# Attention scores: the second matmul of a chunk contracts only the 64 rows that hold the high part of the queries

## The chip, the cores and the metric

The kernel runs on one core of one Trainium2 chip. The metric is the device time in microseconds of one execution, all transfers included. A core has a tensor engine (PE; its weight loads are listed apart as PEld), a vector engine (DVE), a scalar engine (ACT), GpSimd (POOL) and SyncE (SP), which here issues nearly all DMAs.

## The reference

A trunk of two layers over a sequence of 1024 with a width of 1024, in float32: an RG-LRU block and a SwiGLU feed-forward, then stick-breaking attention with 16 heads of 64 and another feed-forward, each with an RMS norm ahead. The change concerns the scores `z` of the attention:

```python
def stick_breaking_attention(x, w_qkv, w_o):
    qkv = jnp.einsum("bsd,de->bse", x, w_qkv).reshape(bsz, seq, 3, N_HEADS, HEAD_DIM)
    ...
    for blk in range(seq // Q_BLOCK):
        ...
        z = jnp.einsum("bhqd,bhkd->bhqk", qb, kb).astype(jnp.float32) * scale
        ...
        log_fail = jnp.where(strict, jax.nn.log_sigmoid(-z), 0.0)
        suffix = lax.cumsum(log_fail, axis=3, reverse=True) - log_fail
        weights = jnp.where(strict, jnp.exp(jax.nn.log_sigmoid(z) + suffix), 0.0)
        outs.append(jnp.einsum("bhqk,bhkd->bhqd", weights.astype(vb.dtype), vb))
    ...
    return jnp.einsum("bse,ed->bsd", o, w_o)
```

## The kernel before

The kernel multiplies in a reduced float32 format (`F32R`). To keep the precision of float32, an operand is held as a high part, rounded to that format, and a low part, what the rounding left over. A full product of two split operands is three matmuls, high by high, high by low and low by high (`mm3`, lines 140 to 143).

**Scores.** A head has only 64 dimensions, half the 128 rows that PE contracts. The kernel uses the free half for the split. For head `hx` (0 or 1) of head pair `q`, the tile `Q[q][hx]` of 128 by 1024 holds the queries' high part in 64 of its rows and their low part in the other 64. For `hx` 0 the high part lies in rows 0 to 63 (`top`), for `hx` 1 in rows 64 to 127 (`bot`). `KH[q][hx]` holds the high part of the keys twice, in both halves, and `KL[q][hx]` the low part of the keys twice. So one matmul of `Q` by `KH` (line 1388) gives high by high and low by high, and a second of `Q` by `KL` into the same PSUM tile (line 1389) adds high by low and low by low. Both have the same stationary operand, a block of 128 queries; each matmul has its own weight load.

**Chunks.** `z_part` computes the scores of one chunk: 128 queries by up to 512 keys. `chunk_list` makes 12 chunks for a head, 192 in all: 96 have 512 columns, 32 have 384 and 64 have 256. `z_rest` then takes the sigmoids (ACT, lines 1408 and 1409), the running product along the keys (DVE scan, lines 1412 and 1414) and the product that gives the weights (POOL, line 1415).

**Order.** PE, ACT, DVE and POOL run in the order in which the program is written (`manual_schedule`). The loop at lines 1527 to 1540 does for each step `u`: the score pair of chunk `u + 8` (`LEAD` is 8), the transposes of the weights for unit `u + 2` (up to four, line 1426) and their split, the rest of the chunk, two steps of filling work, and the two matmuls of weights by values of unit `u` (lines 1447 and 1448). Filling work is mostly `qkv_steps`, the projections of the next head pair, three matmuls of 512 columns a step (lines 141 to 143). All matmuls other than line 1389's keep 128 rows in before and after. Score tiles come from a PSUM pool of two, so a chunk's first matmul waits until ACT has read the chunk two back.

**Moves.** `qkv_steps` makes the queries, keys and values of a head pair in halves of 512 positions. It splits the product into `th` (high) and `tl` (low), each 128 rows for the two heads, and copies 64-row halves into `Q`, `KH` and `KL` by DMAs from SP's queue (`move`, defined at line 1348; each is 64 by 512 float32, 128 KB). For the keys these are eight moves a half, lines 1354 to 1356. `th` and `tl` have one buffer each, so the next split waits until the moves out of it have landed.

Of the kernel before, what the change touches and what calls it, by code (L numbers as in the profile page):

```python
# [33 lines left out]
def trunk(  # L34
# [22 lines left out]
    nc = tc.nc  # L57
# [53 lines left out]
    def load_raw(src, shape):  # L111
        raw = rp.tile([P, D], F32, tag="raw", name="raw")
        view = raw if len(shape) == 1 else raw.rearrange("p (a b) -> p a b", a=shape[0])
        nc.sync.dma_start(view, src)
        return raw
# [11 lines left out]
    def cols(w, c0, n=P):  # L127
        return w[:, c0 : c0 + n].rearrange("(k p) c -> p k c", p=P)
# [11 lines left out]
    def mm3(ps, wh, wl, mh, ml, first, last, **kw):  # L140
        nc.tensor.matmul(ps, lhsT=wh, rhs=mh, start=first, stop=False, **kw)  # L141
        nc.tensor.matmul(ps, lhsT=wh, rhs=ml, start=False, stop=False, **kw)  # L142
        nc.tensor.matmul(ps, lhsT=wl, rhs=mh, start=False, stop=last, **kw)  # L143
# [107 lines left out]
    with ExitStack() as st, tc.manual_schedule(engines={E.PE, E.Activation, E.DVE, E.Pool, E.SP}):  # L251
# [42 lines left out]
        ps = pst("vps0")  # L294
# [49 lines left out]
        ps = pst("vps")  # L344
# [940 lines left out]
    with ExitStack() as st:  # L1285
# [11 lines left out]
        Q, KH, KL, VV = {}, {}, {}, {}  # L1297
        top, bot = slice(0, HD), slice(HD, P)
# [6 lines left out]
        def next_weights(raw):  # L1305
            hi, lo = wtile("whi"), wtile("wlo")
            nc.scalar.copy(hi, raw)
            for i in range(NH):
                later.append(lambda c=half(hi, i), a=half(lo, i), b=half(raw, i): nc.vector.tensor_sub(a, b, f32(c)))
            k3 = lambda t: t.rearrange("p (k c) -> p k c", k=ND)  # L1310
            return k3(hi), k3(lo)
# [3 lines left out]
        def qkv_steps(q):  # L1315
            full = lambda tag: [ap.tile([P, S], F32R, tag=tag, name=tag, bufs=4) for _ in range(2)]
            VV[q] = ap.tile([P, NT, 2, P], F32R, tag="v", name="v", bufs=2)
            for which in range(3):
                w = wq.pop((q, which))
                nx = (q, which + 1) if which < 2 else (q + 1, 0)  # L1320
                if nx[0] < NP:
                    wq[nx] = next_weights(load_raw(cols(w_qkv, nx[1] * D + nx[0] * P), (ND,)))
                else:
                    mix[0].load(0)
                    mix[0].w[mix[0].order[0]] = next_weights(mix[0].raw.pop(0))
                    mix[0].load(1)
                    mix[0].load(2)
                for n in range(NH):
                    ps = psQ.tile([P, NB], F32, tag="qk", name="qk_ps")
                    for k in range(ND):  # L1330
                        mm3(ps, w[0][:, k], w[1][:, k], xh[k][n], xl[k][n], k == 0, k == ND - 1)
                        if k == 3 and late:
                            late.pop()()
                        if k < ND - 1:
                            yield
                    t = ap.tile([P, NB], F32, tag="t", name="t", bufs=2)
                    nc.vector.tensor_mul(t, ps, rbc[n])
                    cs = slice(n * NB, (n + 1) * NB)
                    if which == 0 and n == 0:
                        Q[q] = full("q")  # L1340
                    if which == 1 and n == 0:
                        KH[q], KL[q] = full("kh"), full("kl")
                    if which < 2:
                        th = ap.tile([P, NB], F32R, tag="qh_", name="qh_", bufs=1)
                        tl = ap.tile([P, NB], F32R, tag="ql_", name="ql_", bufs=1)
                        nc.scalar.copy(th, t)
                        nc.vector.tensor_sub(tl, t, f32(th))
                        move = lambda dst, p0, src, p1: nc.sync.dma_start(f32(dst)[p0, cs], f32(src)[p1])
                        for hx, (a, b) in enumerate(((top, bot), (bot, top))):
                            if which == 0:  # L1350
                                move(Q[q][hx], a, th, a)
                                move(Q[q][hx], b, tl, a)
                            else:
                                for dst, src in ((KH[q][hx], th), (KL[q][hx], tl)):
                                    move(dst, top, src, a)
                                    move(dst, bot, src, a)
                    else:

                        def v_turn(n=n, t=t):
                            tp = psQ.tile([P, NB], F32, tag="qk", name="vt_ps")  # L1360
                            for i in range(4):
                                nc.tensor.transpose(tp[:, i * P : (i + 1) * P], t[:, i * P : (i + 1) * P], ident)
                            src = tp.rearrange("p (b h c) -> p b h c", b=4, h=2)
                            bs = slice(4 * n, 4 * n + 4)
                            for hx in range(2):
                                nc.scalar.copy(VV[q][:, bs, hx, 0:HD], src[:, :, hx])
                                nc.vector.tensor_sub(
                                    VV[q][:, bs, hx, HD:P], src[:, :, hx], f32(VV[q])[:, bs, hx, 0:HD]
                                )

                        late.append(v_turn)
                    yield
# [11 lines left out]
        def z_part(q, hx, j, ci, c0, c1, diag):  # L1384
            nk = (j + 1) * P
            ps = psZ.tile([P, NB], F32, tag="z", name="z_ps")
            lhsT = Q[q][hx][:, j * P : (j + 1) * P]
            nc.tensor.matmul(ps[:, 0 : c1 - c0], lhsT=lhsT, rhs=KH[q][hx][:, c0:c1], start=True, stop=False)  # L1388
            nc.tensor.matmul(ps[:, 0 : c1 - c0], lhsT=lhsT, rhs=KL[q][hx][:, c0:c1], start=False, stop=True)  # L1389
            return ps  # L1390


# [97 lines left out]
        def all_fill():  # L1490
            yield from first
            for q in range(1, NP):
                yield from qkv_steps(q)
            for q, n in od:
                nc.sync.dma_start(f32(xh[q][n]), od[q, n][0])
                nc.sync.dma_start(f32(xl[q][n]), od[q, n][1])
            yield
            yield
            late.pop()()
            qs.close()  # L1500
            mix[0].proc(1)
            po = pos.enter_context(tc.tile_pool(name="fpo", bufs=1, space=PSUM, side="right", reuse_waits="tile"))
            ob = po.tile([P, S], F32, name="ob")
            mix.append(ob)
            for _ in range(2):
                yield
            for i, d in enumerate(mix[0].order[:2]):
                w = mix[0].w[d]
                for k in range(ND - 1):
                    mm3(ob[:, i * NB : (i + 1) * NB], w[0][:, k], w[1][:, k], xh[k][0], xl[k][0], k == 0, False)  # L1510
                    yield
                    yield
# [4 lines left out]
        with tc.manual_schedule(engines={E.PE, E.Activation, E.DVE, E.Pool}):  # L1517
            sts, first = stats_steps(), qkv_steps(0)


            for i in range(2 * ND * NH):
                if i >= 5:
                    next(sts, None)
                next(first)
                if i >= 5 and later:
                    later.pop(0)()
            for u in range(-LEAD, len(units)):
                c = u + LEAD
                if c < len(chunks):
                    z = z_part(*chunks[c])  # L1530
                if 0 <= u + 2 < len(units):
                    ready[u + 2] = t_split(t_part(*units[u + 2]), *units[u + 2])
                if c < len(chunks):
                    z_rest(z, *chunks[c])
                if later:
                    later.pop(0)()
                for _ in range(2):
                    next(fill, None)
                if u >= 0:
                    av_part(ready.pop(u), *units[u])  # L1540
            while later:
                later.pop(0)()
# [49 lines left out]
```

## Time and profile before

| | us |
|---|---|
| median of 2 runs | 2209.22 |
| lowest and highest | 2208.43, 2210.01 |
| profiled execution | 2209.81 |
| its span in the trace | 2207.9 |
| stage with the score matmuls | 994 to 1466 of the span |

The busy times of the engines in the trace are sums of recorded lengths. Matmuls are pipelined: a recorded length reaches past the start of the next matmul, and its end is modelled. What a matmul takes from PE is seen in the distance of starts. In rows of the order of time, the columns are start in us, length in us, engine, line, operation, what is written from what, shapes and count; in brackets stands idle time of that engine before it, and what ended it. In the answer for a line, lengths are least, median and greatest in ns.

### The profile page before, as it was taken

Reading aid. Unit: us, or ns where it says so; the run is one execution under the profiler, and the core shown is the slowest. Engines: PE = TensorE matmul, PEld = TensorE weight load, DVE = VectorE, ACT = ScalarE, POOL = GpSimd, SP = SyncE. Lnnn points to the kernel's source line nnn. Section 1 sums busy time; section 2 is a strip of 40 time slices with the busy share of each in tenths; the row PEclk is TensorE's granted clock in tenths of the full one; section 3 lists DMA queues with packets and bytes.
Section 4 is the critical chain, followed back from the end, with each engine's and each line's share of the span. In section 5 each row is a group of like instructions: output and inputs, shape, how many; then the busy total and the mean of one; then the engine's idle time right before and its main releaser. Section 6 shows DMA issues by size and latency. Waiting matters only on the chain.

```text
span 2207.9 us, 28478 instructions
## 1 busy us (share of the span) xinstructions
PE 2176.5 (99%) x10120; PEld 1805.7 (82%) x10120; DVE 1709.9 (77%) x2383; ACT 1150.2 (52%) x2007; POOL 287.2 (13%) x379
## 2 busy tenths in 40 slices
PE   7999999999999999999999999989999999999998
PEld 6888888888888888878888888878888888888887
DVE  6887778767777887878888888876876777788876
ACT  5577435343444544546666666653533444454556
POOL 2222020000000000003334333321000000000002
PEclk9999999999999999999999999989999999999999
DMA  7111412334444764444333333532133444467442
GB/s 230 48 48 39 134 39 72 102 123 158 143 149 134 261 209 122 148 136 98 89 94 96 105 87 104 177 128 70 39 110 124 148 148 133 154 225 234 137 152 86
DMA packets 298702, 277.72 MB, mean 126 GB/s; under 512 B 16312, under 2 KB 215104, under 8 KB 298560
## 3 DMA queue, kind: packets, MB, share of 16 engines
q1 hardware_dynamic: 298544, 275.91, 40.1%
q8 instruction: 79, 1.29, 0.2%
q14 instruction: 63, 0.52, 0.1%
q10 hardware_dynamic: 16, 0.00, 0.0%
HBM read 175.71 MB, written 74.97 MB: 114 GB/s over the span
## 4 chain that ended last, share of the span: by engine, by line
PE 88%; DVE 6%; ACT 3%; DMA 1%; issue 1%; SPq 1%; DVEq 0%; ACTq 0%
PE p_ps L143 18%; PE p_ps L141 18%; PE p_ps L142 18%; PE qk_ps L143 3%; PE qk_ps L141 3%; PE qk_ps L142 3%; PE wt_ps L1426 3%; PE ob_ps L142 2%; PE ob_ps L141 2%; PE ob_ps L143 2%; PE a_ps L143 2%; PE a_ps L142 2%; PE a_ps L141 2%; PE z_ps L1388 1%; DVE F L1414 1%; PE z_ps L1389 1%
## 5 line engine op out<-in xcount | busy, mean ns | idle before, releaser
L1415 POOL TENSOR_TENSOR w<-w,F 128x128 f32<-128x128 f32 (+1 forms) x192 | 183.7, 957 | 311.1 <-DVE F L1412 159.0
L143 PE MATMUL p_ps<-vh,wcl 128*128 128x512 f32 x524 | 204.2, 390 | 0.5 <-DVE wcl L682 0.5
L143 PE MATMUL p_ps<-vh,wbl 128*128 128x512 f32 x524 | 204.4, 390 | 0.3 <-DVE wbl L672 0.2
L143 PE MATMUL p_ps<-vh,wal 128*128 128x512 f32 x524 | 204.1, 389 | 0.1
L141 PE MATMUL p_ps<-vh,wbh 128*128 128x512 f32 x524 | 204.2, 390 | 0.0
L141 PE MATMUL p_ps<-vh,wch 128*128 128x512 f32 x524 | 204.1, 389 | 0.0
L142 PE MATMUL p_ps<-vl,wbh 128*128 128x512 f32 x524 | 203.9, 389 | 0.0
L142 PE MATMUL p_ps<-vl,wch 128*128 128x512 f32 x524 | 203.9, 389 | 0.0
L141 PE MATMUL p_ps<-vh,wah 128*128 128x512 f32 x524 | 203.9, 389 | 0.0
L142 PE MATMUL p_ps<-vl,wah 128*128 128x512 f32 x524 | 203.9, 389 | 0.0
L668 ACT CAST wbh<-sb 128x1024 fp32r<-128x1024 f32 (+2 forms) x69 | 69.6, 1009 | 193.7 <-DVE sb L652 193.6
L212 POOL TENSOR_TENSOR acc<-acc,rbc 128x512 f32<-128x512 f32 x30 | 40.4, 1348 | 773.6 <-ACT rbc L211 773.6
L1436 DVE TENSOR_TENSOR tl<-wt_ps,th 128x512 fp32r<-128x512 f32 x192 | 106.0, 552 | 39.2 <-ACT th L1435 37.1
L1435 ACT CAST th<-wt_ps 128x512 fp32r<-128x512 f32 x192 | 92.5, 482 | 83.1 <-PE wt_ps L1426 82.0
L141 PE MATMUL qk_ps<-vh,whi 128*128 128x512 f32 x264 | 118.6, 449 | 0.7 <-ACT vh L215 0.7
L143 PEld LDWEIGHTS p_ps<-vh,wbl 128*128 128x128 f32 x524 | 98.3, 188 | 22.3 <-DVE wbl L672 2.0
L143 PEld LDWEIGHTS p_ps<-vh,wcl 128*128 128x128 f32 x524 | 98.4, 188 | 21.9 <-DVE wcl L682 1.6
L143 PEld LDWEIGHTS p_ps<-vh,wal 128*128 128x128 f32 x524 | 98.4, 188 | 21.3 <-DVE wal L663 1.0
L142 PEld LDWEIGHTS p_ps<-vl,wah 128*128 128x128 f32 x524 | 98.4, 188 | 20.6
L142 PEld LDWEIGHTS p_ps<-vl,wch 128*128 128x128 f32 x524 | 98.4, 188 | 20.5
L142 PEld LDWEIGHTS p_ps<-vl,wbh 128*128 128x128 f32 x524 | 98.4, 188 | 20.5
L141 PEld LDWEIGHTS p_ps<-vh,wbh 128*128 128x128 f32 x524 | 98.4, 188 | 20.3 <-ACT ta L1053 0.2
(400 smaller groups left out, 5851.2 us busy)
## 6 DMA issues: line engine op xcount, KB each, us to landing
raw<-in_ffn_w_in SPq DMA_DIRECT2D x88, 512.0 KB, 3.8
vl<-pd SPq DMA_DIRECT2D x128, 256.0 KB, 3.6
pd<-U SPq DMA_DIRECT2D x90, 256.0 KB, 2.3
raw<-in_ffn_w_out SPq DMA_DIRECT2D x56, 256.0 KB, 3.9
raw<-in_attn_w_qkv SPq DMA_DIRECT2D x24, 512.0 KB, 3.8
raw<-in_lru_w_in SPq DMA_DIRECT2D x16, 512.0 KB, 4.1
acc<-pd SPq DMA_DIRECT2D x28, 256.0 KB, 2.6
pph<-rbc SPq DMA_DIRECT2D x28, 256.0 KB, 2.5
```

What stands on the lines that cost most here:

```text
L141: nc.tensor.matmul(ps, lhsT=wh, rhs=mh, start=first, stop=False, **kw)
L142: nc.tensor.matmul(ps, lhsT=wh, rhs=ml, start=False, stop=False, **kw)
L143: nc.tensor.matmul(ps, lhsT=wl, rhs=mh, start=False, stop=last, **kw)
L212: (eng or nc.gpsimd).tensor_add(acc[n], acc[n], sq)
L668: nc.scalar.copy(self.full(self.wb), self.full(self.sb))
L1388: nc.tensor.matmul(ps[:, 0 : c1 - c0], lhsT=lhsT, rhs=KH[q][hx][:, c0:c1], start=True, stop=False)
L1389: nc.tensor.matmul(ps[:, 0 : c1 - c0], lhsT=lhsT, rhs=KL[q][hx][:, c0:c1], start=False, stop=True)
L1414: nc.vector.tensor_tensor_scan(rev, rev, rev, first, op0=ALU.mult, op1=ALU.bypass)
L1415: nc.gpsimd.tensor_mul(wt, wt, F[:, 1 : n + 1])
L1426: nc.tensor.transpose(tp[:, c : c + P], W[q, hx, j, kb // 4][:, (kb % 4) * P : (kb % 4 + 1) * P], ident)
L1435: nc.scalar.copy(th[:, q0:], tp[:, q0:])
L1436: nc.vector.tensor_sub(tl[:, q0:], tp[:, q0:], f32(th)[:, q0:])
```

## The change

The second matmul of a chunk takes only the 64 rows of `Q` that hold the high part of the queries, and the same 64 rows of `KL`. It adds high by low, and no longer low by low. The low part of the keys is then needed in one half only, so it is moved once and not twice.

```diff
-                                for dst, src in ((KH[q][hx], th), (KL[q][hx], tl)):
-                                    move(dst, top, src, a)
-                                    move(dst, bot, src, a)
+                                move(KH[q][hx], top, th, a)
+                                move(KH[q][hx], bot, th, a)
+                                move(KL[q][hx], a, tl, a)
...
             nc.tensor.matmul(ps[:, 0 : c1 - c0], lhsT=lhsT, rhs=KH[q][hx][:, c0:c1], start=True, stop=False)
-            nc.tensor.matmul(ps[:, 0 : c1 - c0], lhsT=lhsT, rhs=KL[q][hx][:, c0:c1], start=False, stop=True)
+            a = (top, bot)[hx]
+            nc.tensor.matmul(ps[:, 0 : c1 - c0], lhsT=lhsT[a], rhs=KL[q][hx][a, c0:c1], start=False, stop=True)
```

Here `a` is `top` for head 0 of a pair and `bot` for head 1. The allocations of `KL`, the number and order of the matmuls and everything else stay.

## The prediction

> **What bounds the kernel now.** I read the page's head, busy times and chain of waits first, to see which engine sets the end:
>
> ```profile
> span 2207.9 us, 28478 instructions
> PE 2176.5 (99%) x10120; PEld 1805.7 (82%) x10120; DVE 1709.9 (77%) x2383; ACT 1150.2 (52%) x2007; POOL 287.2 (13%) x379
> PE 88%; DVE 6%; ACT 3%; DMA 1%; issue 1%; SPq 1%; DVEq 0%; ACTq 0%
> ```
>
> PE is busy 99% of the span and carries 88% of the chain. The change touches the attention stage only, so I next took the stage that holds all the score matmuls, in the view of stretches, and the waits of PE and of its weight loads (PEld) inside it:
>
> ```profile
> core 0: us, PE busy (x) PEld busy (x) DVE busy (x) ACT busy (x) POOL busy (x), PEclk, DMA share, GB/s
> 994.00:1466.00 472.00, 465.43 (x2471) 391.04 (x2471) 397.07 (x571) 312.82 (x760) 185.55 (x317) 0.99 0.39 107
> ```
>
> ```profile
> PE ob L141 <- issue: 3.9, 1, 3.9
> PE z_ps L1388 <- ACT w L1409: 2.5, 7, 0.4
> PEld z_ps L1388 <- ACT w L1409: 4.9, 7, 0.8
> ```
>
> The stage takes 472 us and PE is busy for 465.4 of them at a granted clock of 0.99. DVE has 397, ACT 313, and the DMA engines are at 39%. PE waits for others only a few microseconds: one stop of 3.9 us, and seven short ones where a score matmul waits for a score buffer. So time that PE gains or loses in this stage reaches the end nearly one for one, while work taken off DMA, DVE or ACT does not.
>
> **The change, part by part.** The answer for line 1389 says what the edit acts on:
>
> ```profile
> L1389 PEld LDWEIGHTS z_ps<-kl,q x192: 186/187/333, 994.7 to 1464.7; 128*128 128x128 f32 x192
> L1389 PE MATMUL z_ps<-kl,q x192: 278/392/628, 994.7 to 1464.9; 128*128 128x512 f32 x96, 128*128 128x256 f32 x64, 128*128 128x384 f32 x32
> ```
>
> There are 192 of these matmuls, and each has a weight load of its own. The change removes none of them: the count, the 512, 256 or 384 columns that are streamed, and the 128 columns of weights all stay. Only the rows go from 128 to 64.
>
> *Does a matmul of half the rows stream faster, or load faster?* What a matmul takes of PE is the distance from its start to the next start, since the recorded lengths overlap. In order of time:
>
> ```profile
> 1072.18 0.39 PE L1448 MATMUL av_ps<-tl,v 128*128 128x512 f32 x1
> 1072.41 0.39 PE L1388 MATMUL z_ps<-kh,q 128*128 128x512 f32 x1
> 1072.41 0.19 PEld L1389 LDWEIGHTS z_ps<-kl,q 128*128 128x128 f32 x1
> 1072.64 0.39 PE L1389 MATMUL z_ps<-kl,q 128*128 128x512 f32 x1
> 1072.64 0.14 PEld L1426 LDWEIGHTS wt_ps<-ident,w 128*128 128x128 f32 x1
> 1072.87 0.27 PE L1426 MATMUL wt_ps<-ident,w 128*128 128x128 f32 x1
> ...
> 1203.20 0.28 PE L1388 MATMUL z_ps<-kh,q 128*128 128x256 f32 x1
> 1203.31 0.28 PE L1389 MATMUL z_ps<-kl,q 128*128 128x256 f32 x1
> 1203.43 0.27 PE L1426 MATMUL wt_ps<-ident,w 128*128 128x128 f32 x1
> ...
> 1204.92 0.34 PE L1447 MATMUL av_ps<-th,v 128*128 128x384 f32 x1
> 1205.10 0.34 PE L1448 MATMUL av_ps<-tl,v 128*128 128x384 f32 x1
> ```
>
> 512 columns take 0.23 us, 384 take 0.18, 256 take 0.11: PE's time goes by columns, which the change leaves alone. The one load of few rows in the trace, of the transpose of the first gains, is this:
>
> ```profile
> 2.24 0.18 PEld L295 LDWEIGHTS vps<-ident,vmix 8*128 8x128 f32 x1 [2.24 <-POOL ident masks.py:199]
> ```
>
> 8 rows of weights take 0.18 us against 0.187 for 128 rows, so a load of 64 rows is not shorter by anything that counts. Both terms are zero gain.
>
> *What hides the loads, and can go.* In the rows above, the load for L1389 starts at 1072.41, in the moment in which the matmul L1388 starts, and lies wholly beside it; likewise the load for the transpose beside L1389. Both neighbours fill the same 128 rows. The trace also shows a load without that cover, after one of the seven waits:
>
> ```profile
> 1205.80 0.44 PE L1388 MATMUL z_ps<-kh,q 128*128 128x384 f32 x1 [0.37 <-ACT w L1409]
> 1205.80 0.19 PEld L1388 LDWEIGHTS z_ps<-kh,q 128*128 128x128 f32 x1 [0.68 <-ACT w L1409]
> 1205.91 0.19 PEld L1389 LDWEIGHTS z_ps<-kl,q 128*128 128x128 f32 x1
> 1206.08 0.34 PE L1389 MATMUL z_ps<-kl,q 128*128 128x384 f32 x1
> ```
>
> From L1388 to L1389 it is 0.28 us here, where 384 columns take 0.18 under cover: an uncovered load costs 0.10. (The next load starts 0.11 after it, which is the same thing.)
>
> After the change PE goes from 128 rows to 64 and back in every chunk, because what follows a score pair is a transpose, a projection or a weights-times-values matmul, all of 128 rows. That is 2 x 192 = 384 changes of the row count. No row of before shows PE change its row count between two matmuls in a stream, so the price of one change has to be bounded. Low end: 0, if the narrow load still goes under the wide matmul and the reverse. Next: 0.10, if the load must wait for the running matmul's columns to be through. High end: the load waits until the running matmul has fully ended. The recorded length of 512 columns is 0.39 and the distance 0.23, so a matmul has a tail of 0.16 that the next one now overlaps; 0.10 + 0.16 = 0.26. With the load at its whole recorded 0.19, it is 0.35. Below zero is excluded for a change of rows as such, since it takes no column away; the only gain, matmuls side by side, is a rival below.
>
> I take 0.18: the uncovered load, 0.10, which the trace shows, and half the tail, 0.08, because the ends of matmuls are modelled and the true tail may be shorter. Between 0 and 0.26 it is nearest to the row at 1205.80, and I choose that row over the covered ones because all covered loads have neighbours of equal rows, and none has what the change makes.
>
> The Trainium skill's page "TensorEngine Tiling (Array Packing)", section Tiling Modes, Key Properties, speaks for a price: "Changing tiling mode (not just tile) drains the TensorE", and lists 64 rows as a mode other than 128. It names no time; by it the sum would lie with the load and a full tail, and no run so far shows it.
>
> So 384 x 0.18 = 69.1 us, all on PE, which is the path.
>
> *What takes some of it back.* The seven waits of L1388 for ACT (at most 4.9 us, by the loads) are places where PE runs ahead of DVE and ACT. A PE that is 0.36 us later in each chunk no longer arrives early there: I take off the whole 4.9. Nothing else becomes late: DVE, at 397 of 472 us, gets more room, and scores are computed eight chunks ahead of their use.
>
> *The moves of the keys.* Per head pair and half of the sequence, four moves of the low part become two: 2 x 2 x 8 = 32 moves less, each 128 KB.
>
> ```profile
> L1348 SPq DMA_DIRECT2D kl<-ql__7721 x4: 462/570/597, 991.7 to 995.1; - x4
> 994.28 0.28 PE L1388 MATMUL z_ps<-kh,q 128*128 128x256 f32 x1
> 994.66 0.19 PEld L1389 LDWEIGHTS z_ps<-kl,q 128*128 128x128 f32 x1 [0.41 <-issue]
> 994.70 0.36 PE L1389 MATMUL z_ps<-kl,q 128*128 128x256 f32 x1
> 995.97 0.62 ACT L1346 CAST qh__7759<-t 128x512 fp32r<-128x512 f32 x1 [5.53 <-DMA kh<-qh__7720]
> ```
>
> At 0.57 us of issue this is some 18 us of SP's queue, and 4 MB of transfers, beside PE's work. The moves are late only once, at the first chunk: its low-part load sits idle 0.41 us, and there the removed move lets the needed one land one issue earlier. Gain: 0.4 us. The cast of the next keys at 995.97 waits 5.5 us for the last high-part move and will wait about 0.6 less, but PE was not waiting for it. If this hidden part were worth more, it would be by some tenths more at that one place.
>
> Sum: 69.1 - 4.9 - 0.4 = +63.8 us. The profiled execution took 2209.81 us, of which 2207.9 is span; the median shown is 2209.22, 0.6 below, and the sum is made in differences, so it goes onto the median: 2209.2 + 63.8 = 2273 us, 2.9% slower. 2% of the time, about what a measurement of this kernel can tell from no change, is 44.2 us, which is reached from (44.2 + 5.3) / 384 = 0.13 us for a change of rows.
>
> **The rivals.**
>
> *The cover stays (other side: not slower).* PE loads the 64 rows of weights while the 128-row matmul still streams, as it does now at 1072.41, and the wide load under the narrow matmul. For it: PE already goes from score matmuls to transposes, another kind of matmul, at 1072.64 to 1072.87 with no more than the 0.23 of the columns. Against it: that change leaves the rows as they are. It would decide whenever narrow and wide loads are treated as equal ones are. Price 0; result 2209.2 - 0.4 = 2209 us. The Trainium skill's page "TensorE: Matmul & The Clock Gate", Part 2, step 1, would have it so: loads are pulled ahead of matmuls in flight when the row groups don't conflict or when they go to a background weight buffer. That the trace has loads beside matmuls of the same rows agrees with the second of these; whether it holds between modes no run here shows.
>
> *Only the load is laid bare.* The load waits for the columns, not for the tail: 384 x 0.10 - 5.3 = +33 us, 2242 us, 1.5% and within the 2%. For it: this is exactly the price at 1205.80, where nothing was in flight ahead. Against it: a machine that refuses to load beside a matmul of other rows has a reason to let that matmul end first.
>
> *Half the array left free.* The narrow matmul runs beside a neighbour and its columns cost nothing: 96 x 0.23 + 32 x 0.18 + 64 x 0.11 = 34.9 us less, 2174 us, still within 2%. Against it: both neighbours need all 128 rows, so there is no free half to run in. Nearly excluded.
>
> That the change doesn't do what it says, with 128 rows fed all the same, would give the time of the first rival and be seen in the shapes.
>
> **How the numbers follow.** Forecast, load and part or all of the tail: 0.53. The cover stays: 0.30. Load alone: 0.14, of which 0.02 comes out above the 2%. Side by side: 0.03, of which 0.01 goes past 2%, in case more than the second matmul's columns are gained. So slower 0.55, within 2% 0.44, faster 0.01. The predicted time is the forecast's, 2273. Its own range goes from the 2% point, 2254, to 384 x 0.35 - 5.3 = +129, 2338. The range for 8 in 10 must take in the cover case, 2209, with its scatter (the runs go from 2208.4 to 2210.0), so from 2206; above, it goes past load and full tail, 384 x 0.26 - 5.3 = +94.5 or 2304, to 0.29 a change, 2315. Left out are the side-by-side case and the upper end of the forecast, together under 2 in 10.
>
> **What would show it.** The stretch that now is 994 to 1466 gets about 64 us longer, and the stages before and after keep their lengths. In the order of time, the load of L1389, with 64 rows, starts no longer at the start of L1388 but after its columns; L1388 to L1389 is about 0.41 us instead of 0.23, and L1389 to the next of PE too. If these distances stay at 0.23 the cover stays, and the first rival is right; at 0.33 it is the load alone; at 0.49 the full tail. The seven waits for ACT are gone or shorter. Wrong too would be a growth that lies on DVE or in DMA, with the distances as they were, or a granted clock that falls from 0.99 in this stretch because PE pauses.

## The result and the profile after

The changed kernel takes 2264.99 us (2263.95 to 2266.04) against 2209.22 us: 2.55% more, ratio 1.0255 with a 95% interval of 1.0230 to 1.0279. The profiled execution took 2266.04 us. The page, head, busy times and chain:

```profile
span 2264.3 us, 28402 instructions
PE 2239.0 (99%) x10120; PEld 1801.3 (80%) x10120; DVE 1703.4 (75%) x2383; ACT 1153.1 (51%) x2007; POOL 287.1 (13%) x379
PE 93%; DVE 3%; ACT 1%; DMA 1%; issue 0%; SPq 0%; POOL 0%; DVEq 0%; ACTq 0%
```

The span is 56.4 us longer, PE's busy time 62.5 us, with the same 10120 matmuls. The busy times of DVE, ACT and POOL are within 7 us of what they were. The chain has moved further onto PE, from 88% to 93%.

The answers for the two score matmuls (line 1389 of before is line 1390 now), and the waits of weight loads in the attention stage:

```profile
L1388 PE MATMUL z_ps<-kh,q x192: 275/387/628, 992.5 to 1522.9; 128*128 128x512 f32 x96, 128*128 128x256 f32 x64, 128*128 128x384 f32 x32
L1390 PEld LDWEIGHTS z_ps<-kl,q x192: 182/183/285, 992.7 to 1523.2; 64*128 64x128 f32 x192
L1390 PE MATMUL z_ps<-kl,q x192: 378/491/792, 992.7 to 1523.2; 64*128 64x512 f32 x96, 64*128 64x256 f32 x64, 64*128 64x384 f32 x32
```

```profile
PEld z_ps L1390 <- issue: 47.7, 163, 0.4
PEld wt_ps L1427 <- issue: 22.1, 90, 1.8
PEld wt_ps L1427 <- DVE F L1413: 6.6, 27, 0.2
```

The shapes show that 64 rows are contracted. From the first L1388 to the last second matmul it is now 992.5 to 1523.2, 530.7 us, where before it was 994.3 to 1464.9, 470.6 us: +60.1 us, all of the loss. The granted clock in this stretch is 0.99, as before. (The first score matmul lies 1.8 us earlier in this execution, ahead of anything the change touches, and the time after the last one is 1.9 us shorter.) New are idle times of the weight loads ahead of L1390 and of the transpose behind it, with no engine waited for ("issue"; DVE F is named beside it only because it was the last to finish). Gone is the wait of L1388 for ACT, 4.9 us before.

Where a chunk's time goes, in order of time, for 512 columns and one transpose behind. After:

```profile
1114.61 0.39 PE L1449 MATMUL av_ps<-tl,v 128*128 128x512 f32 x1
1114.84 0.39 PE L1388 MATMUL z_ps<-kh,q 128*128 128x512 f32 x1
1115.15 0.50 PE L1390 MATMUL z_ps<-kl,q 64*128 64x512 f32 x1
1115.15 0.18 PEld L1390 LDWEIGHTS z_ps<-kl,q 64*128 64x128 f32 x1 [0.36 <-issue]
1115.58 0.33 PE L1427 MATMUL wt_ps<-ident,w 128*128 128x128 f32 x1
1115.58 0.14 PEld L1427 LDWEIGHTS wt_ps<-ident,w 128*128 128x128 f32 x1 [0.25 <-issue]
1115.67 0.48 PE L141 MATMUL qk_ps<-vh,whi 128*128 128x512 f32 x1
1115.98 0.40 PE L142 MATMUL qk_ps<-vl,whi 128*128 128x512 f32 x1
```

The same place of before goes on, behind the rows from 1072.18 to 1072.87 in the prediction, with:

```profile
1072.90 0.47 PE L141 MATMUL qk_ps<-vh,whi 128*128 128x512 f32 x1
1073.21 0.39 PE L142 MATMUL qk_ps<-vl,whi 128*128 128x512 f32 x1
```

From the weights-times-values matmul to L142 it is 1.37 us after and 1.03 before: 0.34 us for two changes of rows. L1388 to L1390 is 0.31 instead of 0.23. L1390 to the transpose is 0.43 instead of 0.23. The transpose to L141 is 0.09 instead of 0.03. The load for L1390 starts at 1115.15, when the 0.23 us of L1388's columns have been over for 0.08 us, and no longer beside L1388; the transpose's load likewise starts only when its matmul does. 192 x 0.34 = 65.3 us, of which the stage shows 60.1: 5.2 us came back.

That chunk is typical. Set side by side matmul by matmul, the two traces show 0.34 us more in the mean of 185 chunks, from L1388 to the matmul behind the transposes. In the seven chunks that in before followed a wait for ACT it is 0.15 us, because their loads were bare (uncovered) there already, as at 1205.80 in the prediction. The starts of these seven chunks, no longer waiting, give 3.7 us back.

### The profile page after: what moved, and what is told of

Its sections match the earlier page's. It is cut to its first block, busy times and chain, and to the rows that moved or that the text cites. A ratio compares the mean times of both kernels' runs of the same rounds, so it can differ in the third digit from the quotient of the medians.

```text
span 2264.3 us, 28402 instructions
## 1 busy us (share of the span) xinstructions
PE 2239.0 (99%) x10120; PEld 1801.3 (80%) x10120; DVE 1703.4 (75%) x2383; ACT 1153.1 (51%) x2007; POOL 287.1 (13%) x379
## 4 chain that ended last, share of the span: by engine, by line
PE 93%; DVE 3%; ACT 1%; DMA 1%; issue 0%; SPq 0%; POOL 0%; DVEq 0%; ACTq 0%; POOLq 0%
PE p_ps L143 17%; PE p_ps L141 17%; PE p_ps L142 17%; PE wt_ps L1427 4%; PE qk_ps L141 4%; PE qk_ps L143 4%; PE qk_ps L142 4%; PE z_ps L1390 3%; PE ob_ps L142 2%; PE ob_ps L141 2%; PE ob_ps L143 2%; PE a_ps L142 2%; PE a_ps L141 2%; PE a_ps L143 2%; PE z_ps L1388 2%; PE av_ps L1449 2%
## 5 line engine op out<-in xcount | busy, mean ns | idle before, releaser
L141 PE MATMUL p_ps<-vh,wbh 128*128 128x512 f32 x524 | 204.2, 390 | 0.0
L141 PE MATMUL p_ps<-vh,wch 128*128 128x512 f32 x524 | 204.1, 389 | 0.0
L142 PE MATMUL p_ps<-vl,wbh 128*128 128x512 f32 x524 | 203.9, 389 | 0.0
L142 PE MATMUL p_ps<-vl,wch 128*128 128x512 f32 x524 | 203.9, 389 | 0.0
L141 PE MATMUL p_ps<-vh,wah 128*128 128x512 f32 x524 | 203.9, 389 | 0.0
L142 PE MATMUL p_ps<-vl,wah 128*128 128x512 f32 x524 | 203.9, 389 | 0.0
L141 PE MATMUL qk_ps<-vh,whi 128*128 128x512 f32 x264 | 119.0, 451 | 0.6 <-ACT vh L215 0.6
L141 PEld LDWEIGHTS p_ps<-vh,wbh 128*128 128x128 f32 x524 | 98.4, 188 | 20.5 <-ACT ta L1053 0.2
L141 PEld LDWEIGHTS p_ps<-vh,wah 128*128 128x128 f32 x524 | 98.4, 188 | 20.5
L141 PEld LDWEIGHTS p_ps<-vh,wch 128*128 128x128 f32 x524 | 98.4, 188 | 20.4
L142 PEld LDWEIGHTS p_ps<-vl,wbh 128*128 128x128 f32 x524 | 98.4, 188 | 20.3
```

## The experiments

The theory: each passage between 128 and 64 rows costs PE a wait past the columns of the running matmul and a bare weight load, one that no running matmul covers. Rivals: the price belongs to the narrow matmul itself; to the moves of the keys; to the number of rows as such. Each time is compared with executions of the kernel before on the same chip, whose median was 2206.7 to 2207.9 us there.

**The moves alone undone.** The narrow matmul stays, the low part of the keys is moved into both halves again.

```diff
-                                move(KL[q][hx], a, tl, a)
+                                move(KL[q][hx], top, tl, a)
+                                move(KL[q][hx], bot, tl, a)
```

> Narrow second matmul as in the change, but the low part of the keys is moved into both halves as before, so the moves are those of before. If the time comes from the change of row count on PE: 2264 to 2266 us, as the changed kernel, because the moves lie beside PE. If part of the loss or gain comes from the moves: the difference to 2265 is their worth; a loss by moves would bring it back towards 2209.

Measured: 2265.55 us, ratio 1.0264 (1.0249 to 1.0280). The loss is all there with the moves of before. The moves are not its cause, and dropping 32 of them gains nothing that shows.

**The matmul alone undone.** The moves of the change, but 128 rows, and zeros in the half that is not moved.

```diff
                         KH[q], KL[q] = full("kh"), full("kl")
+                        nc.gpsimd.memset(f32(KL[q][0])[bot], 0.0)
+                        nc.gpsimd.memset(f32(KL[q][1])[top], 0.0)
...
-            a = (top, bot)[hx]
-            nc.tensor.matmul(ps[:, 0 : c1 - c0], lhsT=lhsT[a], rhs=KL[q][hx][a, c0:c1], start=False, stop=True)
+            nc.tensor.matmul(ps[:, 0 : c1 - c0], lhsT=lhsT, rhs=KL[q][hx][:, c0:c1], start=False, stop=True)
```

> The moves of the change, but the second matmul contracts all 128 rows, and the half of the low keys that is not moved is filled with zeros by GpSimd. Same sum as the changed kernel, same row count everywhere. Change of row count is the cause: about 2209 us, all of the loss gone, the 0.23 us from L1388 to the next matmul of 512 columns back. If dropping moves or the order of the moves were the cause: about 2265. If GpSimd's memsets hold up the keys of a pair: 2211 to 2220.

> The kernel with the zero half once more, with more rounds, to see whether the 2.9 us below the kernel before are real. If 32 moves less are worth something: ratio 0.9985 to 0.9995 with an interval below 1. If it was scatter: 1.000 within 0.001.

Measured: 2205.06 us, ratio 0.9988 (0.9979 to 0.9998), and the second time 2206.02 us, 0.9994 (0.9985 to 1.0003). The loss is gone, with the same moves and the same sum as the changed kernel. In order of time (L1390 and L1391 are here the two score matmuls):

```profile
1100.42 0.39 PE L1450 MATMUL av_ps<-tl,v 128*128 128x512 f32 x1
1100.65 0.39 PE L1390 MATMUL z_ps<-kh,q 128*128 128x512 f32 x1
1100.88 0.39 PE L1391 MATMUL z_ps<-kl,q 128*128 128x512 f32 x1
1101.11 0.27 PE L1428 MATMUL wt_ps<-ident,w 128*128 128x128 f32 x1
1101.14 0.47 PE L141 MATMUL qk_ps<-vh,whi 128*128 128x512 f32 x1
```

0.23 us from start to start throughout. GpSimd's 16 memsets (0.95 us each) hold up nobody: no engine's wait in the trace is put down to them. Whether fewer moves are worth a tenth of a per cent stays open, since one interval of the two reaches past 1. This version is as fast as before or slightly faster, and clearly faster than the change.

**The narrow matmul twice.**

```diff
-            nc.tensor.matmul(ps[:, 0 : c1 - c0], lhsT=lhsT[a], rhs=KL[q][hx][a, c0:c1], start=False, stop=True)
+            nc.tensor.matmul(ps[:, 0 : c1 - c0], lhsT=lhsT[a], rhs=KL[q][hx][a, c0:c1], start=False, stop=False)
+            nc.tensor.matmul(ps[:, 0 : c1 - c0], lhsT=lhsT[a], rhs=KL[q][hx][a, c0:c1], start=False, stop=True)
```

> The narrow matmul is issued twice in a row on the same 64 rows (high by low is added twice). Price on the change of row count: the second narrow matmul has its load covered again and costs its columns alone, 96 x 0.23 + 32 x 0.18 + 64 x 0.11 = 35 us, so 2265 + 35 = 2300 us, and narrow to narrow is 0.23 us for 512 columns. Price on each narrow matmul, wherever it stands (0.32 us a chunk in after): 2300 + 192 x 0.32 = 2361 us, or with half of it for each, 2330.

Measured: 2299.22 us, ratio 1.0413 (1.0396 to 1.0431). That is 34 us over the changed kernel, the columns alone. In order of time (L1390 and L1391 are the two narrow ones):

```profile
1105.72 0.40 PE L1388 MATMUL z_ps<-kh,q 128*128 128x512 f32 x1
1106.05 0.49 PE L1390 MATMUL z_ps<-kl,q 64*128 64x512 f32 x1
1106.38 0.39 PE L1391 MATMUL z_ps<-kl,q 64*128 64x512 f32 x1
1106.71 0.66 PE L1428 MATMUL wt_ps<-ident,w 128*128 128x128 f32 x4
...
1106.04 0.18 PEld L1390 LDWEIGHTS z_ps<-kl,q 64*128 64x128 f32 x1 [0.26 <-issue]
1106.15 0.19 PEld L1391 LDWEIGHTS z_ps<-kl,q 64*128 64x128 f32 x1
```

The second narrow load starts 0.11 us after the first and lies beside the first narrow matmul: between equal row counts the cover is there, at 64 rows as at 128. The start of L1390 is that of its bare load, so 0.33 from L1390 to L1391 is 0.10 of load and 0.23 of columns; that the expectation named 0.23 for this distance overlooked this. From L1391 to the transpose it is 0.33 again, 0.23 of columns and 0.10 of waiting. The price lies on the change.

**Half of the changes.** Only head 0 of each pair is narrow.

```diff
-            nc.tensor.matmul(ps[:, 0 : c1 - c0], lhsT=lhsT, rhs=KL[q][hx][:, c0:c1], start=False, stop=True)
+            a = slice(0, HD) if hx == 0 else slice(0, P)
+            nc.tensor.matmul(ps[:, 0 : c1 - c0], lhsT=lhsT[a], rhs=KL[q][hx][a, c0:c1], start=False, stop=True)
```

> Only head 0 of each pair has the narrow second matmul (rows 0 to 63), head 1 contracts 128 rows; moves as before. Half the changes of row count: 61 / 2 = 30.5 us on PE, less 2 to 5 us that the waits for ACT give back: 2235 to 2238 us. If it is rows 64 to 127 alone that cost: 2209. If rows 0 to 63 alone cost: 2265.

Measured: 2232.85 us, ratio 1.0114 (1.0099 to 1.0130), 24.9 us over the before of its call and a little below the expected range. In the stage, from the first to the last score matmul, it is 991.3 to 1487.3, 496.0 us, 25.4 over before. 192 changes cost less than half of the 57.6 us that the 384 of the kernel with all moves cost. What comes back does not halve with the price: 96 x 0.34 = 32.6, less 25.4, is 7.2 here against 5.2, of which the starts of L1388 that no longer wait for ACT give 3.7 in both. Neither half of the rows pays alone, which would have given 2209 or 2265 us.

**96 rows in place of 64.** As above, with `slice(0, 96)` for head 0.

> As the kernel with head 0 alone narrow, but with 96 rows (0 to 95) in place of 64; 32 rows of the low queries take part again. If any change of the number of rows costs: 2235 to 2238 us, as with 64 rows in head 0. If what costs is going between tilings of the array (full, half, quarter), and 96 rows run as a full array: 2208 to 2211 us, and L1388 to the next is 0.23 us.

Measured: 2208.31 us, ratio 1.0006 (0.9996 to 1.0016). No price at all, and the load is covered:

```profile
1111.41 0.33 PE L1388 MATMUL z_ps<-kh,q 128*128 128x256 f32 x1
1111.58 0.28 PE L1390 MATMUL z_ps<-kl,q 96*128 96x256 f32 x1
1111.70 0.38 PE L1427 MATMUL wt_ps<-ident,w 128*128 128x128 f32 x2
...
1111.35 0.19 PEld L1388 LDWEIGHTS z_ps<-kh,q 128*128 128x128 f32 x1
1111.46 0.19 PEld L1390 LDWEIGHTS z_ps<-kl,q 96*128 96x128 f32 x1
```

The load of 96 rows starts ahead of L1390, beside L1388, and the 256 columns take their 0.12. (The 0.17 from L1388 to L1390 stands at this chunk in before too.) So it isn't a change of the number of rows as such that costs.

**32 rows.** `a` is rows 0 to 31, for head 1 rows 64 to 95.

> The second matmul contracts 32 rows (the first half of a head's dimensions; the other half of high by low is left out). The same 384 changes, now between full array and 32 rows. Price on the change of tiling, whatever its size (0.34 us a chunk in after): 2262 to 2268 us, and L1388 to L1390 again 0.09 past the columns. If the price follows the rows that are dropped (64 rows less cost 58 us, so 96 rows less cost 87): about 2295; if a shorter load pays: below 2260.

Measured: 2266.56 us, ratio 1.0268 (1.0254 to 1.0282), the same as with 64. The same distances too, to 0.01 us:

```profile
1108.01 0.39 PE L1388 MATMUL z_ps<-kh,q 128*128 128x512 f32 x1
1108.33 0.49 PE L1390 MATMUL z_ps<-kl,q 32*128 32x512 f32 x1
1108.75 0.55 PE L1427 MATMUL wt_ps<-ident,w 128*128 128x128 f32 x3
```

96 rows go as 128, and 64 and 32 pay the same. That fits the Trainium skill, "TensorEngine Tiling (Array Packing)", section Tiling Modes, which has row tilings of 128, 64 and 32 and says that a change between them drains the engine; 96 is no tiling of its own. That it is the tiling, and not something else that 64 and 32 share, follows from this list and not from the runs alone.

**The narrow matmul first.**

```diff
-            nc.tensor.matmul(ps[:, 0 : c1 - c0], lhsT=lhsT, rhs=KH[q][hx][:, c0:c1], start=True, stop=False)
             a = (top, bot)[hx]
-            nc.tensor.matmul(ps[:, 0 : c1 - c0], lhsT=lhsT[a], rhs=KL[q][hx][a, c0:c1], start=False, stop=True)
+            nc.tensor.matmul(ps[:, 0 : c1 - c0], lhsT=lhsT[a], rhs=KL[q][hx][a, c0:c1], start=True, stop=False)
+            nc.tensor.matmul(ps[:, 0 : c1 - c0], lhsT=lhsT, rhs=KH[q][hx][:, c0:c1], start=False, stop=True)
```

> The narrow matmul goes first in the chunk and the wide one second: the row count falls after a matmul of the filling or of weights by values, and rises between the two score matmuls. The same 384 changes. If each change is a wait of 0.09 past the columns and a bare load of 0.10 to 0.11, where after hid most of the second load in the transposes' own pace (bare loads cost four transposes 0.03 only): 192 x (0.20 + 0.20) = 77 us less 5, 2281 us. If the price of a change does not depend on what follows: 2265.

Measured: 2270.23 us, ratio 1.0296 (1.0281 to 1.0311), between the two figures. The distances are those of the theory (L1389 is the narrow one):

```profile
1110.42 0.39 PE L1449 MATMUL av_ps<-tl,v 128*128 128x512 f32 x1
1110.74 0.49 PE L1389 MATMUL z_ps<-kl,q 64*128 64x512 f32 x1
1111.16 0.50 PE L1390 MATMUL z_ps<-kh,q 128*128 128x512 f32 x1
1111.50 0.49 PE L1427 MATMUL wt_ps<-ident,w 128*128 128x128 f32 x3
```

0.32, 0.42 and 0.34 in place of three times 0.23: 0.39 us a chunk, where 0.40 was expected and 0.34 is paid with the wide matmul first. But the stage, 992.5 to 1529.5, grew by 66.4 us only, of 192 x 0.39 = 75. What follows a change does matter, by 5 to 6 us in all. The expectation put the bare load ahead of four transposes at 0.03 us; in the changed kernel's trace it is 0.06. That more came back here than the waits for ACT hold is seen and not explained.

**Two chunks at a time.**

```diff
-                if c < len(chunks):
-                    z = z_part(*chunks[c])
+                if c < len(chunks) and c % 2 == 0:
+                    zs = [z_part(*chunks[c + i]) for i in range(2)]
+                    for i in range(2):
+                        z_low(zs[i], *chunks[c + i])
```

Here `z_part` has the wide matmul alone, and `z_low` the narrow one.

> Two chunks at a time: wide, wide, narrow, narrow, every second step; the same matmuls, half the changes of row count (192). Price on the change: 96 x 0.32 = 31 us, less up to 5: 2235 to 2240 us, if PE does not wait for ACT to free the two score tiles (each such wait is seen at L1388). Price on each narrow matmul: 2265 or more.

Measured: 2260.37 us, ratio 1.0251 (1.0236 to 1.0266). The expected gain of about 28 us did not come. The waits of the weight loads say why:

```profile
PEld z_ps L1388 <- ACT w L1413: 28.5, 51, 1.8
PEld z_ps L1394 <- issue: 18.4, 64, 0.4
PEld wt_ps L1430 <- issue: 18.2, 50, 1.9
```

The idle time ahead of the narrow load fell from 47.7 to 18.4 us, so fewer changes did cost less. But two chunks take both score tiles at once, and the load of L1388 now waits 28.5 us for ACT to read them, in 51 places. On PE itself, the distances from the first to the second wide matmul of the 96 pairs hold 24 us more than the columns take in before. A new wait took the place of the price. So this run does not measure the price of half the changes; head 0 alone does.

## Why the prediction was right

*The bound.* PE set the end of the stage, and its time reached the end nearly one for one: 65.3 us by the distances in a chunk, 60.1 in the stage, 55.8 in the medians.

*No gain from fewer rows.* Right: a load of 64 rows is recorded at 0.183 us and one of 128 at 0.187 to 0.188, and 512 columns of the narrow matmul come to 0.23 as well, once the 0.10 of its load or of the wait behind it is taken off 0.33 (the rows of the narrow matmul twice).

*The price of a change.* The forecast was 0.18 us for each; it was 0.17. The two parts are those of the prediction, a bare load and a wait past the columns. That the size came so near is partly luck: of the recorded tail of 0.16 half was taken, without a row that said half. The wait past the columns is 0.08 to 0.09, and the bare load about 0.11. The two changes of a chunk are unequal: 0.19 to 0.20 going in, and 0.14 to 0.15 coming out, since the bare load ahead of a transpose lengthens what follows by 0.06 only; put before the wide matmul, coming out costs about 0.20 too. The wait does not grow with the columns: for 256 columns L1388 to L1390 has 0.09 to spare, as the rows at 1103.16 and 1103.36 of the changed kernel show beside 0.11 to 0.12 before:

```profile
1103.16 0.28 PE L1388 MATMUL z_ps<-kh,q 128*128 128x256 f32 x1
1103.36 0.38 PE L1390 MATMUL z_ps<-kl,q 64*128 64x256 f32 x1
```

*What takes some back.* 4.9 us were forecast from the waits for ACT. They are gone from the trace, and 5.2 us are missing in the stage: 3.7 by the starts of L1388, and most of the rest in those seven chunks, where bare loads were nothing new. Behind the last score matmul a further wait became shorter, which the prediction had at nothing (below, at the sum).

*The moves.* Forecast 0.4 us of gain; no median separates it from nothing. The stop at the first chunk is indeed gone: 0.42 us from L1388 to L1389 before, 0.20 in the changed kernel. But with the moves of before and the narrow matmul it is 0.21, so it did not go because moves were dropped.

*The sum.* 63.8 us were forecast and 55.8 measured; against the medians of before in the later calls, the same narrow matmul cost 57.6. The price was over by 69.1 - 65.3 = 3.8 us. The rest of the difference lies outside the stretch of the score matmuls, where this execution and that of before differ by 3.7 us. Of these, 1.8 us lie ahead of it, where the change does nothing. Of the 1.9 us behind it, 1.2 are a wait of PE for DVE that the slower PE shortens. The first line is of before, the second of the changed kernel, each from the last score matmul on:

```profile
PE wt_ps L1426 <- DVE tl L1436: 2.7, 2, 1.6
PE wt_ps L1427 <- DVE tl L1437: 1.5, 1, 1.5
```

It is 1.5 us with 32 rows too, and 2.7 with the zero half, so it goes with the price and is not scatter.

*What would show it.* One mark was set wrong: L1388 to L1390 was to become 0.41 us in the case of the forecast, and became 0.31, which by the marks is nearer to the load alone (0.33). In these rows a matmul's recorded start is that of its bare load (both 1115.15), so the load's part shows in the next distance, 0.43. The sum of the two, 0.74, lies between the 0.66 of the load alone and the 0.82 announced; the 0.06 more at the transpose bring a chunk to 0.80.

*The rivals.* That the cover stays, which had a chance of 0.30, fell with the load at 1115.15, which no longer starts beside L1388. The page "TensorE: Matmul & The Clock Gate" of the Trainium skill, Part 2, by which loads go ahead to a background buffer, holds here between matmuls of 128 rows and between matmuls of 64, and not from one to the other. That only the load is laid bare fell with the 0.08 us past the columns. Matmuls side by side were not seen.

## What to carry to other kernels

Contracting fewer rows saved PE nothing by itself, since its time went by columns, and a matmul of 64 or 32 rows amid matmuls of 128 cost about 0.17 us at each passage, here 384 times. Fill the unused rows with zeros, or with terms that do no harm, when the neighbours are full; or bring the narrow matmuls together, but count the PSUM tiles that this holds at once. To price such an edit, look at whether the next weight load still starts beside the running matmul.

## What the runs showed of the hardware that was not expected

A matmul of 96 rows among those of 128 costs nothing (1.0006, 0.9996 to 1.0016, in head 0 alone), where 64 rows in head 0 alone cost 1.1% of this kernel's time. In both heads, 64 and 32 rows cost the same 2.6 to 2.7%. A passage waits 0.08 to 0.09 us past the columns, about half of the tail of 0.16 us by which a matmul's recorded length exceeds its columns.
